# Seven products for the gates and the next values of an mLSTM layer

## Chip, cores and metric

The kernel runs on one core of a Trainium2 chip. The metric is device time in microseconds (us). The kernel before takes 2154.1 us, the median of three runs (2154.06 to 2154.34).

## What is computed

Two layers of an encoder, for 256 positions of width 2048, in float32. Layer 0 mixes by pooling and attention, layer 1 by an mLSTM with 8 heads of 256, and each is followed by a gated MLP with a convolution over positions. The change is in the mixer of layer 1. Cut to what matters, and with both directions in one formula, it is:

```
xn = rms_norm(x, g)                                  # 256 x 2048
q, k, v, o, gates = split(xn @ w_in)                 # 4 x 2048 columns, and 32 for the gates' pre-activations
for each head h (256 columns):
    A = sum over directions of  (q_h k_h^T * decay) / max(|row sum|, bound)      # 256 x 256
    y_h = rms_norm(A @ v_h) * sigmoid(o_h)
x = x + concat(y_h) @ w_out
```

`v` and `o` (the output gates) are thus two products of the same `xn` with two sets of weight columns.

## The kernel before, in words

**Products.** Every large product is made of tiles of 128 rows (K tiles, 16 for a width of 2048) by 512 columns. Both factors are split in a high and a low part that TensorE multiplies at its fp32r rate, and a product takes three matmuls: high by high, high by low, low by high. A group `mv` (values of two heads, 512 columns, 256 positions in two halves t) or `mo` (their gates) takes 16 K tiles x 2 halves x 3 = 96 matmuls into one PSUM tile of the pool `mm`. `mq` and `mk` (queries and keys of one head, L374) have the weights as the stationary side and work likewise.

**Weights.** All weights stream through one list of chunks of 128 x 1024 (512 KB, two K tiles of 512 columns), class Stream. SP loads a chunk into one of 7 buffers `w`, ahead of its use; ACT casts it to the high part (L134) and DVE subtracts that for the low part (L135), into one of 4 buffers `hl`. A chunk of `mo` or `mv` is used by 12 matmuls. The cast of a chunk can start once the last matmul of the chunk four places ahead of it, which used the same buffer, is done.

**Seven products before the change.** The down products of both MLPs (tile `pp`) already go in seven products of half-sized blocks rather than eight, as Strassen's rule does. Their sums of weights are made by DMA in DRAM, by `premix` (L475, tile `m`): per mix two copies are issued by ACT and three accumulating transfers by POOL, each in two halves, paced by the latest matmul. `Made` chunks of the stream are loaded from these sums.

**The mLSTM layer** (from L766). For each pair of heads hp: the values `mv`; for each of its two heads `mq` and `mk`, and a task `head`; then the gates `mo`, and a task `gated`. The order on PE is that of the code. Tasks are Python generators that the class Weave (L161) runs between the matmuls once a given amount of matmul time has gone by, so that small work of one head stands between the large matmuls of what follows. ACT and DVE take their instructions in an order that a scheduler sets when the program is built.

The task `head` issues 12 matmuls `qk`; on DVE four multiplications by the decay, which also sum rows (L882), three small ones for the reciprocal of the bound (L885 to L887) and four that build the matrix `A` (L889 to L892); then four transposes of `A` on PE (`atr`, L898), their split (`at`, L900 and L901), and 12 matmuls `av`. The task `gated` makes the sigmoid of the gates in the tile `og` (ACT exponential L923, DVE addition L927 and reciprocals L929), multiplies the head's normed result by it (L933) and transposes that (`htr`, L938). Both heads' `head` tasks and the `gated` task of a pair run beside the following large groups: the second head's beside `mo` and the next pair's `mv`.

Of the kernel before, what the change touches and what calls it, by code (L numbers as in the profile page):

```python
# [9 lines left out]
F32 = mybir.dt.float32  # L10
F32R = mybir.dt.float32r
AF = mybir.ActivationFunctionType
# [4 lines left out]
P = 128  # L17
D = 2048
# [198 lines left out]
def trunk(ctx: ExitStack, tc: tile.TileContext, gx, xT, xn, call, catt, cml, weights, mixes, out):  # L217
# [555 lines left out]
    def mlstm_layer(norm, nxt):  # L773
        with ExitStack() as es:
# [145 lines left out]
            def gated(ps, heads):  # L920
                og = t1p.tile([P, 2, len(heads) * MD], F32, tag="og", name=f"og{heads[0]}")
                for t in range(2):
                    a.activation(og[:, t, :], ps[:, t, :], AF.Exp, scale=nrcol[:, t : t + 1])  # L923
                yield 1.2
                for i, h in enumerate(heads):
                    o = og[:, :, i * MD : i * MD + MD]
                    v.tensor_scalar_add(o, o, 1.0)  # L927
                    for t in range(2):
                        tc.keep_in_program_order(v.reciprocal(o[:, t], o[:, t]))  # L929
# [3 lines left out]
                    tc.keep_in_program_order(v.tensor_mul(hn, hn, o))  # L933
# [11 lines left out]
                    done.add(h)  # L945

            hns, done = {}, set()
            wv.add(norm.finish(), 6.0)
            for hp in range(MH // 2):
                vf = t1p.tile([P, 2, 512], F32, tag="vf", name=f"mvf{hp}")  # L950
                for c, n in ((0, MD + 32), (MD, MD)) if hp == 0 else ((0, 512),):
                    ps = mov_group(xx, f"mv{hp}_{c}", n)
                    if hp + c == 0:
                        wv.until(lambda: norm.rcol is not None)
                        wv.add(gates(ps))
                    n = min(n, 512 if hp else MD)
                    for t in range(2):
                        a.activation(vf[:, t, c : c + n], ps[:, t, :n], AF.Copy, scale=norm.rcol[:, t : t + 1])
# [12 lines left out]

            def ready(i):
                wv.until(lambda: set(range(6 + 2 * i)) <= done)
# [4 lines left out]
    def ffn_layer(layer, norm, nxt):  # L978
        with ExitStack() as es:
# [229 lines left out]
def _mov(w):  # L1209

    return w.reshape(-1, 2, P, 512).transpose(0, 2, 1, 3).reshape(-1, P, CH * P)
# [18 lines left out]


def _ml_chunks(w_in, w_out):
    a = []
    for hp in range(MH // 2):
        c = 2 * D + hp * 512
        a.append(_mov(w_in[:, c : c + 512]) if hp else _stat(w_in[:, c + MD : c + 512], range(KT)))
# [5 lines left out]
        a.append(_mov(wo))  # L1242
    return np.concatenate(a), _out_chunks(w_out, ML_PARTS)


def _up_chunks(w):
# [56 lines left out]
    return seq + [("down", c, b) for b in range(2, NB)]  # L1303


def _down_chunks(layer, w):
# [12 lines left out]
    res = [np.concatenate(out)]  # L1319

    def two(a, b):
        return np.concatenate([a, b], axis=2)

    for h in range(2):
        b = w[: 2 * n * P, 1024 * h : 1024 * h + 1024].reshape(n, 2, P, 2, 512)
        b11, b12, b21, b22 = (b[:, k, :, c] for k in range(2) for c in range(2))
        res += [two(b12, b12), two(b11, b22), two(b22, b21), two(b11, b21), two(b22[::2], b22[1::2])]
    return res


# [130 lines left out]
```

## Time and profile before

| | |
|---|---|
| median of 3 runs | 2154.1 us |
| profiled execution, its time | 2154.6 us |
| profiled execution, its span | 2152.7 us |
| PE busy | 2147.7 us, 11400 matmuls |
| DVE, ACT, POOL busy | 1760.0, 1420.2, 250.2 us |
| DMA | 578.31 MB, mean 269 GB/s |

The span is the time from the first to the last instruction of the profiled execution; 1.9 us of its time lie outside. "Busy" counts the time in which an engine executes; PE's matmuls overlap, so that the distance from one to the next is shorter than a matmul's own duration. In an answer of the profile, `out<-in` names the tiles that an instruction writes and reads, and xN counts them. L272 is the one line that issues all large matmuls, so groups are told apart by tile. The chain of waits follows the work that ended last back through whatever released it.

### The profile page before, as it was taken

The page shows a single profiled execution, that of the slowest core. Times are in us where ns is not written, and L with a number is a line of the kernel's source. Part 1 is how long each engine was busy: PE and PEld are TensorE (multiplying, and loading weights), DVE is VectorE, ACT ScalarE, POOL GpSimd, SP SyncE. Part 2 cuts the span into 40 slices and gives each one's busy share as a digit, 9 for nine tenths or more (in the row PEclk, how much of TensorE's full clock was granted, in tenths as well). Part 3 has the DMA queues.
Part 4 walks back from the last instruction along what each step waited for, and adds up shares of the span by engine and source line. Part 5 has one row for each costly group of instructions (what it writes and reads, how often), then busy time and mean ns, then how long its engine had stood idle before and what let it go on. Part 6 is the DMA issues. An engine that isn't in the chain of part 4 may idle for free.

```text
span 2152.7 us, 32117 instructions
## 1 busy us (share of the span) xinstructions
PE 2147.7 (100%) x11400; PEld 1842.3 (86%) x11400; DVE 1760.0 (82%) x2468; ACT 1420.2 (66%) x2171; POOL 250.2 (12%) x318
## 2 busy tenths in 40 slices
PE   9999999999999999999999999999999999999999
PEld 8888888888888888889888888888888888888887
DVE  7786678889988999897777677667888998889988
ACT  6665577777777777666554544457777777777774
POOL 0022112111111110001111111111111000000000
PEclk9999999999999999999999999999999999999999
DMA  9678889899999997778788888988989888778775
GB/s 332 209 213 255 261 250 323 269 328 331 317 330 328 315 287 257 264 259 250 227 252 247 244 247 229 286 240 253 298 280 285 281 266 255 268 254 269 253 250 186
DMA packets 172226, 578.31 MB, mean 269 GB/s; under 512 B 22074, under 2 KB 24930, under 8 KB 172066
## 3 DMA queue, kind: packets, MB, share of 16 engines
q1 hardware_dynamic: 131360, 469.16, 61.3%
q0 software_dynamic: 24544, 61.10, 17.0%
q10 hardware_dynamic: 16162, 46.01, 6.6%
q8 instruction: 89, 1.46, 0.3%
q14 instruction: 71, 0.58, 0.1%
HBM read 574.04 MB, written 86.03 MB: 307 GB/s over the span
## 4 chain that ended last, share of the span: by engine, by line
PE 98%; DVE 1%; issue 0%; ACT 0%; ACTq 0%; DVEq 0%
PE up L272 45%; PE pp L272 16%; PE op L272 8%; PE mv L272 4%; PE mq L272 4%; PE mk L272 4%; PE mo L272 4%; PE qproj L272 3%; PE dn L272 3%; PE kproj L272 1%; PE vproj L272 1%; PE pool L272 1%; PE av L272 1%; PE qk L272 1%; PE xt L323 0%; DVE hl L135 0%
## 5 line engine op out<-in xcount | busy, mean ns | idle before, releaser
L135 DVE TENSOR_TENSOR hl<-w,hl 128x1024 fp32r<-128x1024 f32 (+1 forms) x851 | 1024.0, 1215 | 196.0 <-ACT hl L134 186.1
L134 ACT CAST hl<-w 128x1024 fp32r<-128x1024 f32 (+1 forms) x850 | 872.4, 1046 | 420.6 <-PE up L272 121.5
L272 PE MATMUL up<-xx,hl 128*128 128x512 f32 (+1 forms) x5632 | 993.6, 337 | 0.0
L272 PEld LDWEIGHTS up<-xx,hl 128*128 128x128 f32 x5632 | 867.2, 188 | 129.8
L272 PE MATMUL pp<-hl,s 128*128 128x512 f32 x912 | 226.5, 390 | 0.2
L484 POOL DMA_DIRECT2D m<-m x160 | 128.3, 820 | 798.2 <-PE up L272 304.0
L272 PEld LDWEIGHTS pp<-hl,s 128*128 128x128 f32 x912 | 168.1, 188 | 34.2 <-DVE hl L135 1.4
L272 PE MATMUL pp<-hl,g 128*128 128x512 f32 x684 | 173.9, 390 | 0.0
L272 PEld LDWEIGHTS pp<-hl,g 128*128 128x128 f32 x684 | 125.9, 188 | 24.3
L438 ACT COPY tb_up<-up 128x512 f32<-128x512 f32 x88 | 51.7, 587 | 123.0 <-PE up L272 123.0
L484 POOL DMA_DIRECT2D m<-in_dn x80 | 71.0, 888 | 357.1 <-PE dn L272 121.2
L1010 DVE TENSOR_TENSOR y<-y,z 128x510 f32<-128x510 f32 x88 | 60.7, 689 | 60.2 <-ACT y L1009 60.1
L1009 ACT ACTIVATE y<-tb_up,conv 128x256 f32<-128x256 f32 x176 | 103.7, 589 | 0.0
L439 DVE TENSOR_TENSOR tb_up<-up,tb_up 128x512 f32<-128x512 f32 x88 | 60.8, 691 | 40.6 <-ACT tb_up L438 40.2
L272 PE MATMUL mk<-xx,hl 128*128 128x512 f32 (+1 forms) x512 | 92.2, 337 | 0.0
L272 PE MATMUL mq<-xx,hl 128*128 128x512 f32 (+1 forms) x512 | 92.2, 337 | 0.0
L272 PE MATMUL mv<-hl,xx 128*128 128x512 f32 (+2 forms) x480 | 91.8, 351 | 0.0
L272 PE MATMUL op<-hl,cat 128*128 128x512 f32 x384 | 91.5, 393 | 0.0
L272 PE MATMUL mo<-hl,xx 128*128 128x512 f32 x384 | 90.5, 391 | 0.0
L1007 ACT ACTIVATE z<-tb_up,conv 128x256 f32<-128x256 f32 x176 | 88.3, 502 | 3.2 <-DVE tb_up L1002 2.3
L272 PE MATMUL op<-hl,mcat 128*128 128x512 f32 x384 | 89.5, 392 | 0.0
L272 PEld LDWEIGHTS mq<-xx,hl 128*128 128x128 f32 x512 | 79.2, 188 | 11.6
(233 smaller groups left out, 2135.8 us busy)
## 6 DMA issues: line engine op xcount, KB each, us to landing
w<-in_up SPq DMA_DIRECT2D x352, 512.0 KB, 5.8
w<-in_dn SPq DMA_DIRECT2D x174, 512.0 KB, 5.1
w<-in_m_in SPq DMA_DIRECT2D x124, 512.0 KB, 5.2
m<-in_dn ACTq DMA_DIRECT2D x160, 256.0 KB, 5.9
w<-m SPq DMA_DIRECT2D x80, 512.0 KB, 4.8
w<-in_a_in SPq DMA_DIRECT2D x45, 512.0 KB, 5.6
m<-in_dn POOLq DMA_DIRECT2D x80, 256.0 KB, 7.0
m<-m POOLq DMA_DIRECT2D x160, 128.0 KB, 5.8
```

The costliest lines, as they stand in the source:

```text
L134: (self.nc.vector.tensor_copy if i + c == 0 else self.nc.scalar.copy)(hl[:, 0, c : c + n], w[:, c : c + n])
L135: low = self.nc.vector.tensor_sub(hl[:, 1, c : c + n], w[:, c : c + n], hl[:, 0, c : c + n].bitcast(F32))
L272: last_mm[0] = pe.matmul(out_, lhsT, rhs, start=start, stop=stop, skip_group_check=True)
L438: a.copy(tb, ps[:, :, 1, :])
L439: v.tensor_add(tb, ps[:, :, 0, :], tb)
L484: paced(eng.dma_start(to[p : p + P // 2], src[p : p + P // 2], **kw))
L1007: a.activation(z[:, 0, j, :], u[:, j, :], AF.Copy, scale=cw(tl, 0))
L1009: a.activation(y[:, j, :], u[:, j, :], AF.Identity, scale=cw(tl, 1), bias=cw(tl, 3))
L1010: v.tensor_add(y[:, :, 1:S], y[:, :, 1:S], z[:, 0, :, 0 : S - 1])
```

## The change

For the pairs hp = 0, 1 and 2 a new function `gates_values(hp)` makes the gates of pair hp and the values of pair hp + 1 together, as one product with 1024 columns, in the place where `mo` and the next `mv` stood. The first pair's values and the last pair's gates are made as before.

K tiles 0 to 7 go in four pairs. In each pair the two halves of the positions, the two K tiles and the two sets of 512 columns form a 2 x 2 by 2 x 2 product, which takes seven products (21 matmuls) rather than eight (24). Four of the seven have a sum of blocks of `xn` as stationary factor, and one of the others is added directly into `mo`. K tiles 8 to 15 go directly, two parts of `mo` (ML_DIRECT) and the end of `mv`. A pair of heads thus takes 180 large matmuls rather than 192.

What is new beside these matmuls:

- the tile `mcomb` with the sums of blocks of `xn`, high and low part, made once by a task `combos`, five DVE instructions and one ACT cast for each of four pairs of K tiles;
- the PSUM tiles `mp46`, `mp5` and `mp0`, and the tasks `first` and `second`, which add them up in the SBUF tiles `og` and `vf`: two ACT copies, eight DVE instructions of 512 columns, and two more that add `mv` to `vf`. The task `gated` starts behind `second` and reads `og`;
- 22 chunks of weights rather than 16 for each of the three pairs. 14 of them are used by 6 matmuls each and 8 by 12;
- 12 mixes of a third list, `premix(2)`, for the sums of weights of these chunks. They start in the first MLP, where c = 3 and i = 6. The 20 mixes of the second MLP, `premix(1)`, no longer start at c = 5 and i = 4 of the first MLP, but behind the first pair in the mLSTM layer.

Line numbers shift by 2 or 3: the matmuls stand in L274, the cast in L136, the low part in L137, the task `head`'s lines in 885 to 904.

The diff, without the functions that cut and list the weights on the host:

```
+ML_PAIRS = 4
+ML_DIRECT = (list(range(2 * ML_PAIRS, 12)), list(range(12, KT)))
...
+            comb = actp.tile([P, ML_PAIRS, 2, 4, P], F32R, tag="B1", name="mcomb")
...
+            def combine(j):
+                f = tp.tile([P, 2, S], F32, tag="hn", name=f"mf{j}")
+                pair = norm.xx[:, 2 * j : 2 * j + 2]
+                v.tensor_add(f, pair[:, :, 0].bitcast(F32), pair[:, :, 1].bitcast(F32))
...
+                v.tensor_sub(sf[:, 0:2], g4[:, 0::3], g4[:, 1:2].to_broadcast([P, 2, P]))
+                v.tensor_add(sf[:, 2], sf[:, 1], g4[:, 0])
+                v.tensor_sub(sf[:, 3], g4[:, 2], sf[:, 2])
+                a.copy(comb[:, j, 0], sf)
+                v.tensor_sub(comb[:, j, 1], sf, comb[:, j, 0].bitcast(F32))
...
+            def gates_values(hp):
+                og = t1p.tile([P, 2, 512], F32, tag="og", name=f"og{2 * hp}")
+                vf = t1p.tile([P, 2, 512], F32, tag="vf", name=f"mvf{hp + 1}")
+                x00, x10, x01, x11 = og[:, 0], og[:, 1], vf[:, 0], vf[:, 1]
+                wv.until(lambda: "combos" in done)
...
+                direct(mo, ML_DIRECT[0], (True, True), (False, False))
...
+                for j in js:
+                    xs = [[comb[:, j, i, m] for i in range(2)] for m in (1, 0, 2)] + [x_part(2 * j + 1, 1)]
+                    for n, (ps, x_) in enumerate(zip((p46[:, 0], p46[:, 1], p5, mo[:, 1]), xs)):
+                        if n % 2 == 0:
+                            hl = st.next()
+                        wh, wl = (hl[:, i, n % 2 * 512 : n % 2 * 512 + 512] for i in range(2))
+                        product(ps, x_, wh, wl, n < 3 and j == 0, n < 3 and j == js[-1])
...
+                wv.add(first(), 0.3)
+                direct(mo, ML_DIRECT[1], (False, False), (False, True))
+                p0 = psp.tile([P, 512], F32, tag="ps", name=f"mp0{hp}")
+                for j in js:
+                    hl = st.next()
+                    for n, ps in enumerate((p0, mo[:, 0])):
+                        wh, wl = (hl[:, i, n * 512 : n * 512 + 512] for i in range(2))
+                        product(ps, x_part(2 * j + n, 0), wh, wl, n == 0 and j == 0, j == js[-1])
...
+                wv.add(second(), 0.3)
+                mv = mmp.tile([P, 2, 512], F32, tag="mm", name=f"mv{hp + 1}")
+                for j in js:
+                    if j % 2 == 0:
+                        hl = st.next()
+                    wh, wl = (hl[:, i, j % 2 * 512 : j % 2 * 512 + 512] for i in range(2))
+                    product(mv[:, 0], [comb[:, j, i, 3] for i in range(2)], wh, wl, j == 0, False)
+                for n, kts in enumerate(ML_DIRECT):
+                    direct(mv, kts, (False, n == 0), (n == 1, n == 1))
+                wv.until(lambda: f"g{hp}" in done)
+                for t in range(2):
+                    v.tensor_add(vf[:, t], vf[:, t], mv[:, t])
+                    a.activation(vf[:, t], vf[:, t], AF.Copy, scale=norm.rcol[:, t : t + 1])
+                return vf
...
-                wv.add(gated(mov_group(xx, f"mo{hp}"), [2 * hp, 2 * hp + 1]))
+                if hp < MH // 2 - 1:
+                    vf = gates_values(hp)
+                else:
+                    wv.add(gated(mov_group(xx, f"mo{hp}"), [2 * hp, 2 * hp + 1]))
+                hp == 0 and premix(1, 30.0, 30.0, 0)
...
-                    if layer == 0 and c == len(FCH) - 1 and i == 4:
-                        premix(1, 30.0, 30.0, 0)
+                    if layer == 0 and (c, i) == (len(FCH) - 3, 6):
+                        premix(2, 30.0, 30.0, 0)
```

**Place 1, PE, from the start of the gates of pair 0.** Before, `mo` is the gates, and qk and atr belong to the second head of the pair; the number behind `hl` is the chunk.

```order
L272 MATMUL mo_10207<-hl_10157,xx_2446 128x512 x12
L272 MATMUL mo_10207<-hl_10178,xx_2446 128x512 x12
L272 MATMUL mo_10207<-hl_10210,xx_2446 128x512 x12
L272 MATMUL qk_10271<-hl_k_10204,hl_q_10071 128x256 x12
L272 MATMUL mo_10207<-hl_10237,xx_2446 128x512 x12
L272 MATMUL mo_10207<-hl_10256,xx_2446 128x512 x12
L898 MATMUL atr_10334<-cst,A_10293 128x128 x4
```

The same place on PE now; mp is one of the new PSUM tiles mp46 and mp5.

```order
L274 MATMUL mo_10320<-hl_10267,xx_2446 128x512 x12
L274 MATMUL mo_10320<-hl_10291,xx_2446 128x512 x12
L274 MATMUL mp_10366<-hl_10323,mcomb 128x512 x6
L274 MATMUL qk_10379<-hl_k_10315,hl_q_10181 128x256 x12
L274 MATMUL mp_10367<-hl_10351,mcomb 128x512 x3
L274 MATMUL mo_10320<-hl_10351,xx_2446 128x512 x3
L274 MATMUL mp_10366<-hl_10370,mcomb 128x512 x6
L274 MATMUL mp_10367<-hl_10408,mcomb 128x512 x3
L274 MATMUL mo_10320<-hl_10408,xx_2446 128x512 x3
L274 MATMUL mp_10366<-hl_10419,mcomb 128x512 x6
L901 MATMUL atr_10452<-cst,A_10401 128x128 x4
```

Between qk and atr stood 24 matmuls of two chunks; now 24 matmuls of four chunks stand there, the last of them chunk hl_10419.

**Place 1, DVE, the same head's work between qk and atr.** Before (arg is the decay, den and denr the bounds):

```order
L135 TENSOR_TENSOR hl_10318<-w_10208,hl_10318 128x1024
L882 SCALAR_TENSOR_TENSOR arg_10223,den_10284<-qk_10271,arg_10223 128x128
L882 SCALAR_TENSOR_TENSOR arg_10223,den_10284<-qk_10271,arg_10223 128x256 x2
L882 SCALAR_TENSOR_TENSOR arg_10223,den_10284<-qk_10271,arg_10223 128x128
L885 SCALAR_TENSOR_TENSOR denr_10289<-den_10284 128x4
L886 TENSOR_TENSOR denr_10289<-denr_10289,mc 128x4
L887 RECIPROCAL denr_10289<-denr_10289 128x4
L889 TENSOR_SCALAR A_10293<-arg_10223,denr_10289 128x256
L891 TENSOR_SCALAR A_10293<-arg_10223,denr_10289 128x256
L890 SCALAR_TENSOR_TENSOR A_10293<-arg_10223,denr_10289,A_10293 128x128
L892 SCALAR_TENSOR_TENSOR A_10293<-arg_10223,denr_10289,A_10293 128x128
L135 TENSOR_TENSOR hl_10344<-w_10235,hl_10344 128x1024
```

Now, from the end of the multiplications on:

```order
L888 SCALAR_TENSOR_TENSOR denr_10397<-den_10392 128x4
L137 TENSOR_TENSOR hl_10432<-w_10349,hl_10432 128x1024
L889 TENSOR_TENSOR denr_10397<-denr_10397,mc 128x4
L137 TENSOR_TENSOR hl_10443<-w_10368,hl_10443 128x1024
L890 RECIPROCAL denr_10397<-denr_10397 128x4
L137 TENSOR_TENSOR hl_10462<-w_10406,hl_10462 128x1024
L892 TENSOR_SCALAR A_10401<-arg_10332,denr_10397 128x256
L894 TENSOR_SCALAR A_10401<-arg_10332,denr_10397 128x256
L137 TENSOR_TENSOR hl_10473<-w_10417,hl_10473 128x1024
L893 SCALAR_TENSOR_TENSOR A_10401<-arg_10332,denr_10397,A_10401 128x128
L895 SCALAR_TENSOR_TENSOR A_10401<-arg_10332,denr_10397,A_10401 128x128
```

The eleven instructions of the head stood together; now four low parts of chunks stand among them, the last (hl_10473) ahead of the two that finish `A`. Chunk hl_10473 is the fourth behind hl_10419 (hl_10432, hl_10443 and hl_10462 lie between). Pairs 1 and 2 have the same order.

**Place 2, DVE, the sigmoid of the gates.** Before, behind the end of `mo`:

```order
L927 TENSOR_SCALAR og_10435<-og_10435 128x2x256 x2
L929 RECIPROCAL og_10435<-og_10435 128x256 x2
L135 TENSOR_TENSOR hl_10450<-w_10342,hl_10450 128x1024
L929 RECIPROCAL og_10435<-og_10435 128x256
L135 TENSOR_TENSOR hl_10468<-w_10359,hl_10468 128x1024
L135 TENSOR_TENSOR hl_10489<-w_10405,hl_10489 128x1024
L933 TENSOR_TENSOR hn_10137<-hn_10137,og_10435 128x512
```

Now, from the sums of the task `second` on; hl_10656 is the last chunk of `mv`, and from hl_10677 on the chunks are of the next pair's `mq`:

```order
L1033 TENSOR_TENSOR mvf_10319<-mvf_10319,mp_10563 128x512
L137 TENSOR_TENSOR hl_10656<-w_10597,hl_10656 128x1024
L1033 TENSOR_TENSOR mvf_10319<-mvf_10319,mp_10563 128x512
L137 TENSOR_TENSOR hl_10677<-w_10610,hl_10677 128x1024
L930 TENSOR_SCALAR og_10318<-og_10318 128x2x256 x2
L137 TENSOR_TENSOR hl_10696<-w_10623,hl_10696 128x1024
L932 RECIPROCAL og_10318<-og_10318 128x256 x3
L137 TENSOR_TENSOR hl_10724<-w_10635,hl_10724 128x1024
L1049 TENSOR_TENSOR mvf_10319<-mvf_10319,mv_10609 128x512 x2
L936 TENSOR_TENSOR hn_10247<-hn_10247,og_10318 128x512
```

The reciprocals stood among the low parts of `mv`; now they stand behind the sums, among those of the next `mq`.

More of the change, by code (lines that the diff above doesn't have):

```diff
@@ new lines, in combos, with product, x_part @@
+            def combos():
+                for j in range(ML_PAIRS):
+                    yield from wv.wait(lambda: norm.blocks > j // 2)
+                    combine(j)
+                    yield 8.0
+                done.add("combos")
+            def product(ps, xs, wh, wl, first, last):
+                xh, xl = xs
+                mm(ps, xh, wh, first, False)
+                mm(ps, xh, wl, False, False)
+                mm(ps, xl, wh, False, last)
+                wv.tick(0.68)
+            def x_part(k, t):
+                return [norm.xx[:, k, i, t * P : t * P + P] for i in range(2)]
@@ L1232, in _ml_chunks @@
 def _ml_chunks(w_in, w_out):
-    a = []
+    c = 2 * D
+    a, made = [_stat(w_in[:, c + MD : c + 512], range(KT))], [[], [], []]
+    k0, k1 = 2 * ML_PAIRS * P, ML_DIRECT[1][0] * P
     for hp in range(MH // 2):
-        c = 2 * D + hp * 512
-        a.append(_mov(w_in[:, c : c + 512]) if hp else _stat(w_in[:, c + MD : c + 512], range(KT)))
         for h in (2 * hp, 2 * hp + 1):
@@ L1241, in _ml_chunks, with _ml_weights, some @@
         wo = w_in[:, 3 * D + hp * 512 : 3 * D + hp * 512 + 512]
-        a.append(_mov(wo))
-    return np.concatenate(a), _out_chunks(w_out, ML_PARTS)
+        if hp == MH // 2 - 1:
+            a.append(_mov(wo))
+            continue
+        wv = w_in[:, 2 * D + hp * 512 + 512 : 2 * D + hp * 512 + 1024]
+        s0, s1, r, ba, bb = _seven(np.concatenate([wo[:k0], wv[:k0]], axis=1))
+        for to, e in zip(made, (s0, s1, r)):
+            to.append(e)
+        a += [_mov(wo[k0:k1]), _mov(wo[k1:]), ba, bb, _mov(wv[k0:])]
+    return np.concatenate(a), _out_chunks(w_out, ML_PARTS), [np.concatenate(e) for e in made]
+def _ml_weights(chunks, parts):
+    chunks, mixes = iter(chunks), []
+    def some(n):
+        return [next(chunks) for _ in range(n)]
+    out = some(KT // 4)
+    for hp in range(MH // 2):
+        out += some(KT)
+        if hp == MH // 2 - 1:
+            out += some(KT // 2)
+            continue
+        out += some(len(ML_DIRECT[0]) // 2)
+        for j in range(ML_PAIRS):
+            made = [Made(), Made()]
+            mixes.append([p[hp * ML_PAIRS + j] for p in parts] + [made])
+            out += made
+        out += some(len(ML_DIRECT[1]) // 2 + ML_PAIRS + ML_PAIRS // 2 + (KT - 2 * ML_PAIRS) // 2)
+    return out, mixes
 def _up_chunks(w):
@@ L1303, in _ffn_plan, with _seven, two @@
     return seq + [("down", c, b) for b in range(2, NB)]
+def _seven(w):
+    def two(a, b):
+        return np.concatenate([a, b], axis=2)
+    b = w.reshape(-1, 2, P, 2, 512)
+    b11, b12, b21, b22 = (b[:, k, :, c] for k in range(2) for c in range(2))
+    return [two(b12, b12), two(b11, b22), two(b22, b21), two(b11, b21), two(b22[::2], b22[1::2])]
 def _down_chunks(layer, w):
@@ L1319, in _down_chunks @@
     res = [np.concatenate(out)]
[L1321 to L1322 removed]
     for h in range(2):
[L1325 to L1327 removed]
+        res += _seven(w[: 2 * n * P, 1024 * h : 1024 * h + 1024])
     return res
@@ L1433 @@
     }
+    arrays.update({f"m_s{j}": part for j, part in enumerate(m_made)})
     for l in range(2):
@@ L1454 @@
     vg = [t["m_g"][:, c : min(c + n, m_g.shape[1])] for c in range(0, m_g.shape[1], n)]
-    weights = chunks("a_in") + chunks("a_out") + ffn(0) + vg + chunks("m_in") + chunks("m_out") + ffn(1)
+    m_weights, m_mixes = _ml_weights(chunks("m_in"), [chunks(f"m_s{j}") for j in range(3)])
+    weights = chunks("a_in") + chunks("a_out") + ffn(0) + vg + m_weights + chunks("m_out") + ffn(1)
+    mixes.append(m_mixes)
     with tile.TileContext(nc, schedule_with_timeline_sim=True) as tc:
```

55 lines of the change are left out of this document (43 added, 12 removed).

## The prediction

> **What bounds the kernel now.** I read the page first, then the chain of waits, then the busy time by windows over the three stretches that the change touches, and in them the groups and the timeline.
>
> ```profile
> PE 2147.7 (100%) x11400; PEld 1842.3 (86%) x11400; DVE 1760.0 (82%) x2468; ACT 1420.2 (66%) x2171; POOL 250.2 (12%) x318
> PE   9999999999999999999999999999999999999999
> POOL 0022112111111110001111111111111000000000
> PEclk9999999999999999999999999999999999999999
> PE 98%; DVE 1%; issue 0%; ACT 0%; ACTq 0%; DVEq 0%
> ```
>
> PE is busy in 2147.7 of 2152.7 us, in every slice, at full granted clock, and 98% of the chain is PE. Time is lost or won only by matmuls that go or by stalls of PE. PE is as full in the slices in which POOL makes sums of weights (1 or 2) as in those without (0).
>
> One large matmul's price is read from the chain, where a piece is time from start to start, not from its own duration, which overlaps with the next:
>
> ```profile
> 1065.01 13.60 PE mv L272 x60
> 1160.81 13.60 PE mv L272 x60
> 1256.61 13.60 PE mv L272 x60
> ```
>
> 13.60 / 60 = 0.2267 us for each of 512 columns. A chunk used by 12 matmuls thus lasts 2.72 us on PE, one used by 6 only 1.36.
>
> The three stretches of `mo` and the next `mv`, and the one behind the first of them, by windows (columns: PE, PEld, DVE, ACT and POOL busy, granted clock, DMA share, GB/s):
>
> ```profile
> 1039.60:1087.10 47.50, 47.50 (x226) 39.76 (x226) 35.52 (x54) 22.63 (x30) 7.03 (x9) 1.00 0.83 245
> 1135.40:1182.90 47.50, 47.50 (x226) 39.76 (x226) 35.60 (x54) 22.51 (x30) 7.05 (x9) 1.00 0.82 238
> 1231.00:1278.70 47.70, 47.70 (x227) 39.93 (x226) 35.09 (x55) 22.62 (x30) 7.24 (x9) 1.00 0.80 238
> 1087.00:1111.00 24.00, 24.00 (x141) 20.95 (x140) 13.88 (x15) 13.31 (x17) 3.92 (x5) 1.00 0.85 246
> ```
>
> PE has no gap in them; DVE has 12 us to spare in each.
>
> **The matmuls that go.** Three pairs of heads times 192 - 180 = 12 matmuls, 36 in all: 36 x 0.2267 = 8.16 us. This is all that the change takes from PE.
>
> **The work that DVE and ACT get.** From the groups of the first stretch, and from the additions of the down products, whose form (512 columns, one operand in PSUM) is that of the new ones:
>
> ```profile
> L135 DVE TENSOR_TENSOR hl<-w,hl 128x1024 fp32r<-128x1024 f32 x16 | 19.2, 1211 | 6.4 <-ACT hl L134 6.3
> L134 ACT CAST hl<-w 128x1024 fp32r<-128x1024 f32 x16 | 16.8, 1053 | 19.5 <-PE mo L272 9.1 <-PE mv L272 6.7 <-DVE hn L933 2.4
> L929 DVE RECIPROCAL og<-og 128x256 f32<-128x256 f32 x4 | 6.8, 1733 | 0.0
> ```
>
> ```profile
> L1087 DVE TENSOR_TENSOR acc<-acc,pp x64: 676/680/685, 447.7 to 2125.5; 128x512 f32<-128x512 f32 x64
> L1085 ACT COPY acc<-pp x16: 566/582/588, 330.8 to 1563.0; 128x512 f32<-128x512 f32 x16
> its engine sat idle before it (us, times) until:
>   DVE hl L135: 1.4, 3
> ```
>
> A stretch gets six more chunks and ten more additions. DVE: 35.5 + 6 x 1.21 + 10 x 0.68 = 49.6 us of work for 47.5 - 12 x 0.2267 = 44.8 us of PE. ACT: 22.6 + 6 x 1.05 + 2 x 0.58 = 30.1 us, which fits. DVE's 4.8 us too many can go only into what follows, and the window from 1087 has 24.00 - 13.88 = 10.1 us free. Place 2 of the order shows that this is where the reciprocals (6.8 us) now stand. I count the overflow at nothing; without that cover it is the second rival.
>
> **The wait that the order makes.** At place 1, PE reaches the transposes `atr` of a pair's second head right after chunk hl_10419. The first needs L893, which DVE has behind the low part of hl_10473. The cast of hl_10473 needs the buffer of hl_10419, so it cannot start until PE has finished the very matmuls before `atr`. In before nothing of the kind stood there:
>
> ```profile
> L898 PE MATMUL atr<-cst,A x32: 270/272/273, 1028.0 to 1342.5; 128*128 128x128 f32 x32
> ```
>
> ```profile
> 1049.26 5.64 PE L272 MATMUL mo<-hl,xx 128*128 128x512 f32 x24
> 1052.14 0.35 DVE L889 TENSOR_SCALAR A<-arg,denr 128x256 f32<-128x256 f32 x1
> 1052.21 1.05 ACT L134 CAST hl<-w 128x1024 fp32r<-128x1024 f32 x1 [3.08 <-PE mo L272]
> 1052.41 0.35 DVE L891 TENSOR_SCALAR A<-arg,denr 128x256 f32<-128x256 f32 x1
> 1052.67 0.35 DVE L890 SCALAR_TENSOR_TENSOR A<-arg,denr,A 128x128 f32<-128x128 f32 x1
> 1052.94 0.34 DVE L892 SCALAR_TENSOR_TENSOR A<-arg,denr,A 128x128 f32<-128x128 f32 x1
> 1053.30 1.23 DVE L135 TENSOR_TENSOR hl<-w,hl 128x1024 fp32r<-128x1024 f32 x1
> 1054.44 1.40 DVE L869 SCALAR_TENSOR_TENSOR arg<-G,mc,kml 128x128 f32<-128x128 f32 x4
> 1054.51 0.58 PEld L898 LDWEIGHTS atr<-cst,A 128*128 128x128 f32 x4
> 1054.74 0.60 PE L898 MATMUL atr<-cst,A 128*128 128x128 f32 x4
> ```
>
> `A` was complete at 1053.28 and `atr` came at 1054.74: 1.5 us in hand. From these rows the new wait is worked out, counted from the end of hl_10419's last matmul. The 24 matmuls from 1049.26 are two chunks; the first ends at 1049.26 + 2.72 = 1051.98, and the cast that waits for it starts at 1052.21: 0.23 us. The cast takes 1.05, so it ends at 1.28. DVE comes from the cast of the chunk before (hl_10462), released 1.36 us earlier: its low part starts at about -0.08, the next instruction 1.14 us later (1053.30 to 1054.44), and two halves of `A` take 0.27 each (1052.14 to 1052.67 for two), so DVE is free at 1.60. Then the low part, 1.14, and L893, 0.35: 3.1 us. The weights of a transpose are loaded 0.23 us ahead of it (1054.51 to 1054.74): 3.3 us. The last of the four needs L895, which is done at 3.4, and stands 0.45 us behind the first: no more. I take **3.3 us, three times, 9.9 us**. Ends: 2.8 if DVE is free when the cast ends and nothing is paid for loading weights, 4.0 if DVE is another half low part behind. Queued behind `atr` on PE is everything; the splits of the next four chunks are done meanwhile, so none is late after it.
>
> ACT and DVE take their instructions strictly in order, says the Trainium skill ("TensorE: Matmul & The Clock Gate", "Architectural detail"), and PE may pull only loads of weights ahead. By that rule the stall stands; if the two halves of `A` could pass hl_10473 it would vanish, and the sum would be 2146. In the rows above every instruction of DVE starts behind the one before.
>
> **Edits that I cost at nothing or little.**
>
> `combos`: four times five DVE instructions, two of 512 columns (0.68 each, as L1087), one of 256 (0.35, as L891) and two of 128 (at most that), some 2.4 us each time, at the layer's start. In the row below DVE has 4.8 of 13 us free, before that none (6.00 of 6.00), so a step of the start can be late.
>
> ```profile
> 966.00:972.00 6.00, 6.00 (x49) 6.00 (x48) 6.00 (x15) 4.41 (x11) 0.78 (x1) 1.00 0.74 221
> 972.00:985.00 13.00, 13.00 (x106) 13.00 (x105) 8.17 (x15) 7.44 (x12) 1.51 (x2) 1.00 0.91 179
> ```
>
> I take 0.5 us for that and for the transposes `htr`, which come behind the moved reciprocals; ends 0 and 2.4, one set of `combos` in full.
>
> Loads: six more of 512 KB for each pair, which raises the stretch from 245 to about (245 x 47.5 + 6 x 524) / 44.8 = 330 GB/s.
>
> ```profile
> w<-in_m_in SPq DMA_DIRECT2D x124, 512.0 KB, 5.2
> w<-m SPq DMA_DIRECT2D x80, 512.0 KB, 4.8
> GB/s 332 209 213 255 261 250 323 269 328 331 317 330 328 315 287 257 264 259 250 227 252 247 244 247 229 286 240 253 298 280 285 281 266 255 268 254 269 253 250 186
> ```
>
> Slices of the first MLP run at 330 with PE full, so this fits. Loads land in 5.2 us, and six chunks ahead are 8.2 us even where each lasts 1.36: hidden, at nothing. Were it gone, one load would be late by up to 5.2 us.
>
> Short chunks as such: `pp` lives on chunks of 6 matmuls too and waited for low parts three times, 1.4 us in all. But there they alternate with long ones, and here eight come in a row. At 1.36 us each they leave the cast (1.05) and the low part (1.14) just room; that is why anything put between them, as at place 1, is paid.
>
> The mixes: 12 more, in the first MLP (four copies on ACT's queue and six accumulating transfers on POOL's for each). The 20 of the second MLP start behind the first pair, about 1087, where before the first seven copies were issued from 860 to 960, so 130 to 230 us later. The rows of DMA issues in the windows 860 to 960, 1600 to 1700 and 1950 to 2100:
>
> ```profile
> m<-in_dn ACTq DMA_DIRECT2D x7, 256.0 KB, 5.0
> ```
>
> ```profile
> m<-m POOLq DMA_DIRECT2D x10, 128.0 KB, 5.8
> ```
>
> ```profile
> w<-m SPq DMA_DIRECT2D x12, 512.0 KB, 4.7
> ```
>
> The last sums were made before 1700 and would be by 1930, and the chunks of the last six mixes are loaded from 1950 on: in time. By the page's slices PE doesn't feel such transfers: nothing. If a load did have to wait for its sum, the wait would show whole.
>
> **The sum**, against the profiled execution's 2154.6: - 8.16 + 9.9 + 0.5 = 2156.8. That execution lies 0.5 above the median, so the forecast is **2156.3 us**. Of the ends: - 8.2 + 8.4 + 0 gives 2154.3, - 8.2 + 12.0 + 2.4 gives 2160.3.
>
> **Rivals.**
>
> 1. *No stall: the change does its sum.* Then 2154.1 - 8.2 = 2146, up to 2148 with the small terms. It needs `A` done ahead of `atr`, as in before, where 1.5 us were in hand. Against it: the chain above has no link that depends on a duration being long; even its shortest form is 2.8 us.
>
> 2. *DVE's overflow reaches PE (slower).* The place is the end of the stretch, where reciprocals and sums stand among low parts. If the low parts are already late there, PE waits for each, and the 49.6 - 44.8 = 4.8 us are paid for each pair in place of 3.3 or with part of it: 3 x 4.8 = 14.4, 2154.1 - 8.2 + 14.4 = 2160.3. It decides once the low part of the last `mv` chunk or of the first `mq` chunk ends behind PE's need of it. For it: DVE is short by more than the stall gives back. Against it: `mv` ends with four long chunks (10.9 us of PE for 4.6 us of low parts), and the stall itself lets DVE catch up by 3.3 us.
>
> 3. *The clock falls at the stalls.* Before shows no pause of PE in which this could be seen, only PEclk at 9 throughout. If the clock were halved after each stall for as long as the stall, it would cost 3 x 3.3 / 2 = 5.0 us more: 2161.3. The Trainium skill ("TensorE: Matmul & The Clock Gate", "HAM oscillation") says that gaps of PE over about 3.4 us halve the clock, and that the window runs freely; by its "What's actually happening" the whole window must be idle, which a pause of 3.3 us doesn't fill, and by that the sum stays.
>
> **How the numbers follow.** My forecast has 0.62, rival 1 has 0.08, rival 2 0.22, rival 3 0.03, and 0.05 is for a late load or sum of weights, or more. About 0.2% (4.3 us) is what a measurement of this kernel can tell from no change: faster is below 2149.8, slower above 2158.4. Rival 1 is faster, 0.08. Of the forecast's range 2154.3 to 2160.3 the larger part lies below 2158.4: 0.52 of 0.62, and with it a part of rival 2 where only some of the overflow is paid, 0.04: same 0.56. The rest is slower: 0.36. The range leaves out rival 1 and the worst: 2152.5 to 2162.
>
> **What would show it.** In the profile after: `atr` in pairs 0 to 2 with PE idle about 3.3 us before it, released by DVE's L893 or L895, and a gap of that length between mp46's matmuls and `atr`; 36 fewer matmuls; DVE over 95% busy in the stretch, and the same PE period elsewhere. If PE instead waits before `mv` or `mq` matmuls for `hl` L137, rival 2 holds. PEclk below 9 in these slices would show rival 3. The forecast is wrong at its root if `atr` shows no idle time; that DVE's order or the four buffers were read wrongly would be the reason.

## The result, and the profile after

The changed kernel takes 2161.76 us (median of 6 runs, 2160.82 to 2163.09) against 2154.16 before: the ratio is 1.0035, 95% interval 1.0022 to 1.0048. It is slower, by 7.6 us, where I forecast 2.2 more and called it no change; the time lies just within the range.

The page of the profile after, whose own time is 2162.26 us:

```profile
span 2160.5 us, 32447 instructions
PE 2144.7 (99%) x11364; PEld 1837.2 (85%) x11364; DVE 1804.7 (84%) x2536; ACT 1445.4 (67%) x2199; POOL 305.4 (14%) x390
PEclk9999999999999999999999999999999999999999
PE 92%; DVE 3%; DMA 2%; issue 1%; ACT 1%; ACTq 0%; DVEq 0%; SPq 0%
```

11400 - 11364 = 36 matmuls are gone, as the change says. PE is now idle for 15.8 us, and the chain is no longer PE alone: 3% is DVE and 2% DMA. The clock's digits show nothing: 3.4 us at half clock leave the mean of a slice of 54 us at 0.97. What PE waited for:

```profile
PE atr L901 <- DVE A L893: 8.9, 3, 3.0
PE wps L298 <- DVE pad L702: 1.2, 1, 1.2
PE pp L274 <- DVE hl L137: 1.0, 1, 1.0
PE mk L274 <- DVE hl L137: 0.6, 1, 0.6
PE htr L941 <- DVE hn L936: 0.2, 1, 0.2
```

Only `wps` stood there before:

```profile
PE wps L296 <- DVE pad L700: 1.2, 1, 1.2
```

To see where the time comes from I compare the first starts of the same tiles (the answer per tile has min/median/max of the duration, then first and last start), before and then after:

```profile
L272 PE MATMUL up<-xx,hl x5632: 273/336/580, 256.4 to 2103.5; 128*128 128x512 f32 x98, 128*128 128x256 f32 x97
L272 PE MATMUL mv<-hl,xx x480: 278/389/486, 965.1 to 1278.5; 128*128 128x512 f32 x96, 128*128 128x288 f32 x32, 128*128 128x256 f32 x32
L272 PE MATMUL mo<-hl,xx x384: 387/389/476, 1039.7 to 1352.0; 128*128 128x512 f32 x192
L272 PE MATMUL op<-hl,mcat x384: 387/389/486, 1352.2 to 1442.9; 128*128 128x512 f32 x192
```

```profile
L274 PE MATMUL up<-xx,hl x5632: 273/387/580, 256.2 to 2111.3; 128*128 128x512 f32 x98, 128*128 128x256 f32 x97
L274 PE MATMUL mv<-hl,xx x336: 279/297/390, 967.1 to 1285.5; 128*128 128x512 f32 x72, 128*128 128x288 f32 x48, 128*128 128x256 f32 x48
L274 PE MATMUL mo<-hl,xx x312: 387/390/629, 1042.5 to 1359.9; 128*128 128x512 f32 x156
L274 PE MATMUL op<-hl,mcat x384: 387/390/486, 1360.1 to 1450.8; 128*128 128x512 f32 x192
```

So the first MLP (up to mv) went from 708.7 to 710.9, the start of the mLSTM layer (mv to mo) from 74.6 to 75.4, and the rest of that layer with its three changed stretches (mo to op) from 312.5 to 317.6: + 2.2, + 0.8 and + 5.1, with - 0.3 elsewhere the 7.8 us by which the span grew. The first was at nothing in my sum, the second stood there with 0.5, and of the third my sum had 9.9 - 8.2 = 1.7.

The stall that was. The timeline of the first stretch:

```profile
1054.84 1.52 PE L274 MATMUL mp<-hl,mcomb 128*128 128x512 f32 x6
1056.40 1.04 ACT L136 CAST hl<-w 128x1024 fp32r<-128x1024 f32 x1 [0.30 <-PE mp L274]
1057.27 0.35 DVE L892 TENSOR_SCALAR A<-arg,denr 128x256 f32<-128x256 f32 x1
1057.53 0.35 DVE L894 TENSOR_SCALAR A<-arg,denr 128x256 f32<-128x256 f32 x1
1057.80 1.22 DVE L137 TENSOR_TENSOR hl<-w,hl 128x1024 fp32r<-128x1024 f32 x1
1058.93 0.34 DVE L893 SCALAR_TENSOR_TENSOR A<-arg,denr,A 128x128 f32<-128x128 f32 x1
1059.33 0.95 PE L901 MATMUL atr<-cst,A 128*128 128x128 f32 x4 [2.97 <-DVE A L893]
1059.94 1.63 PE L274 MATMUL mp<-hl,mcomb 128*128 128x512 f32 x3
1061.36 1.48 PE L274 MATMUL mo<-hl,xx 128*128 128x512 f32 x3
```

Chunk's end, cast, the rest of A's first halves, low part, L893, `atr`: the chain of the prediction, 2.97 us long. The last two rows show something else: three matmuls take 1.63 and 1.48 us, and the next piece starts 1.42 us after the first; three take 0.68 elsewhere. The windows (busy time of PE, of PEld, which is PE's loading of weights, of DVE, ACT and POOL; then granted clock, DMA share, GB/s) say why:

```profile
1055.00:1059.30 4.30, 1.36 (x7) 0.78 (x5) 4.25 (x8) 2.10 (x2) 0.00 (x0) 1.00 0.98 202
1059.30:1061.00 1.70, 1.67 (x7) 1.48 (x8) 1.67 (x6) 0.59 (x1) 0.00 (x0) 0.57 1.03 414
1061.00:1063.00 2.00, 2.00 (x6) 1.59 (x5) 0.63 (x1) 0.91 (x2) 0.00 (x0) 0.51 1.02 410
1063.00:1066.00 3.00, 3.00 (x19) 2.64 (x18) 1.72 (x2) 2.52 (x3) 0.77 (x1) 1.00 0.53 180
```

```profile
1251.00:1255.10 4.10, 1.22 (x6) 0.68 (x4) 4.05 (x8) 2.00 (x2) 0.25 (x1) 1.00 0.90 227
1255.20:1257.20 2.00, 2.00 (x11) 1.74 (x12) 1.97 (x6) 0.91 (x2) 0.00 (x0) 1.00 0.87 338
1257.20:1259.20 2.00, 2.00 (x11) 1.63 (x10) 0.57 (x2) 1.93 (x3) 0.00 (x0) 1.00 1.02 416
```

Behind the stall of pair 0 the granted clock is half, for some 3.4 us, and then full again; behind that of pair 2, as long, it stays full. Pair 1 is like pair 0: half from 1158.5 to 1161.9. Two halvings cost 2 x 3.4 / 2 = 3.4 us. The three stretches then add up: - 8.2 + 8.9 + 0.2 + 3.4 = + 4.3 of the 5.1; 0.8 us stay spread over small pieces.

**Theory**: the order at `atr` makes the stall, the stall halves the clock, and the mixes in the first MLP delay its loads. **Rival**: DVE is simply short in the stretches, so that a wait which is taken away comes back.

### The profile page after: what moved, and what is told of

Read it like the earlier page. It is cut to its first block, busy times and chain, and to the rows that moved or that the text cites. A ratio compares the mean times of both kernels' runs of the same rounds, so it can differ in the third digit from the quotient of the medians.

```text
span 2160.5 us, 32447 instructions
## 1 busy us (share of the span) xinstructions
PE 2144.7 (99%) x11364; PEld 1837.2 (85%) x11364; DVE 1804.7 (84%) x2536; ACT 1445.4 (67%) x2199; POOL 305.4 (14%) x390
## 4 chain that ended last, share of the span: by engine, by line
PE 92%; DVE 3%; DMA 2%; issue 1%; ACT 1%; ACTq 0%; DVEq 0%; SPq 0%
PE up L274 43%; PE pp L274 15%; PE op L274 8%; PE mk L274 4%; PE mq L274 3%; PE mo L274 3%; PE qproj L274 3%; PE dn L274 3%; PE mv L274 2%; DVE hl L137 2%; PE mp L274 1%; PE kproj L274 1%; PE vproj L274 1%; DMA w<-in_dn 1%; PE pool L274 1%
## 5 line engine op out<-in xcount | busy, mean ns | idle before, releaser
L137 DVE TENSOR_TENSOR hl<-w,hl 128x1024 fp32r<-128x1024 f32 (+1 forms) x869 | 1047.3, 1217 | 173.3 <-ACT hl L136 161.2
L136 ACT CAST hl<-w 128x1024 fp32r<-128x1024 f32 (+1 forms) x868 | 890.8, 1045 | 398.4 <-PE up L274 110.8
L274 PE MATMUL up<-xx,hl 128*128 128x512 f32 (+1 forms) x5632 | 994.1, 337 | 0.1
L274 PEld LDWEIGHTS up<-xx,hl 128*128 128x128 f32 x5632 | 867.6, 188 | 130.1 <-DVE hl L137 0.9
L486 POOL DMA_DIRECT2D m<-m x208 | 166.4, 817 | 943.0 <-PE up L274 428.5
L274 PE MATMUL pp<-hl,s 128*128 128x512 f32 x912 | 227.0, 391 | 1.3 <-DVE hl L137 1.0
L274 PEld LDWEIGHTS pp<-hl,s 128*128 128x128 f32 x912 | 168.0, 188 | 35.9 <-DVE hl L137 3.3
L274 PE MATMUL pp<-hl,g 128*128 128x512 f32 x684 | 174.0, 390 | 0.0
L274 PEld LDWEIGHTS pp<-hl,g 128*128 128x128 f32 x684 | 125.9, 188 | 24.4
L274 PE MATMUL mk<-xx,hl 128*128 128x512 f32 (+1 forms) x512 | 93.2, 338 | 0.6 <-DVE hl L137 0.6
L274 PE MATMUL mq<-xx,hl 128*128 128x512 f32 (+1 forms) x512 | 92.2, 338 | 0.0
L274 PE MATMUL op<-hl,cat 128*128 128x512 f32 x384 | 91.6, 393 | 0.0
L1118 ACT ACTIVATE z<-tb_up,conv 128x256 f32<-128x256 f32 x176 | 88.2, 501 | 3.9 <-DVE tb_up L1113 2.0
L274 PEld LDWEIGHTS mk<-xx,hl 128*128 128x128 f32 x512 | 79.2, 189 | 12.3 <-DVE hl L137 1.0
L274 PE MATMUL op<-hl,mcat 128*128 128x512 f32 x384 | 89.5, 392 | 0.0
L274 PEld LDWEIGHTS mq<-xx,hl 128*128 128x128 f32 x512 | 79.3, 188 | 11.6
L1119 ACT ACTIVATE z<-tb_up,conv 128x256 f32<-128x256 f32 x176 | 87.3, 496 | 0.0
```

Of the source, the lines that this page charges most:

```text
L136: (self.nc.vector.tensor_copy if i + c == 0 else self.nc.scalar.copy)(hl[:, 0, c : c + n], w[:, c : c + n])
L137: low = self.nc.vector.tensor_sub(hl[:, 1, c : c + n], w[:, c : c + n], hl[:, 0, c : c + n].bitcast(F32))
L274: last_mm[0] = pe.matmul(out_, lhsT, rhs, start=start, stop=stop, skip_group_check=True)
L486: paced(eng.dma_start(to[p : p + P // 2], src[p : p + P // 2], **kw))
L1118: a.activation(z[:, 0, j, :], u[:, j, :], AF.Copy, scale=cw(tl, 0))
L1119: a.activation(z[:, 1, j, :], u[:, j, :], AF.Copy, scale=cw(tl, 2))
```

## The experiments

Each time is beside runs of the kernel before on the same chip (2154.0 to 2154.3). The runs of one kernel spread over 2 to 8 us, those of before over 0.3 to 3, so medians tell 1 to 2 us apart at best; finer readings are of one profile each, by the three spans from start to start.

| kernel | median us | ratio, interval | up to mv | mv to mo | mo to op |
|---|---|---|---|---|---|
| before | 2154.2 | | 708.7 | 74.6 | 312.5 |
| changed | 2161.8 | 1.0022 to 1.0048 | 710.9 | 75.4 | 317.6 |
| a_first | 2154.7 | 0.9992 to 1.0011 | 712.7 | 76.4 | 307.9 |
| fill | 2160.3 | 1.0019 to 1.0038 | 710.2 | 76.0 | 314.5 |
| mix_only | 2157.1 | 1.0005 to 1.0024 | 711.9 | 74.5 | 312.6 |
| mix_mid | 2159.2 | 1.0014 to 1.0033 | 709.1 | 76.0 | 313.9 |
| pin_av | 2150.2 | 0.9971 to 0.9990 | 710.7 | 76.0 | 305.0 |
| combos_late | 2161.9 | 1.0023 to 1.0051 | 713.6 | 75.9 | 316.2 |
| best_mid | 2151.9 | 0.9980 to 0.9998 | 709.1 | 76.4 | 308.4 |
| best2 | 2150.7 | 0.9977 to 0.9995 | 709.1 | 76.8 | 307.0 |
| best3 | 2155.2 | 0.9998 to 1.0016 | 709.1 | 83.5 | 306.5 |
| fill4 | one run, 2162.8 | | 712.9 | 75.8 | 316.0 |
| best4 | 2153.7 | 0.9990 to 1.0008 | 709.1 | 79.8 | 306.5 |
| combos_only | 2154.4 | 0.9995 to 1.0013 | 708.6 | 74.6 | 312.5 |

**a_first.** The low part of the third chunk to be split after A's instructions is issued is tied behind them:

```
+                last = v.scalar_tensor_tensor(A[:, 1, P:S], ...)
+                if hh == 1 and h < 6:
+                    st.pin = st.n_split + 2, last
...
+            if self.pin and i >= self.pin[0]:
+                self.behind(low, self.pin[1])
+                self.pin = None
```

> The changed kernel with one order on DVE pinned: at the second head of pairs 0 to 2 the four instructions that build A stand together ahead of the low part of hl_10432 (and its like), as they did before the change; nothing else is touched. Theory (the atr wait is made by the order, and it drags the clock down): PE no longer waits at atr (8.9 us gone) and the granted clock stays 1.00 (3.4 us gone), 2161.8 - 12.3 = about 2149.5. Rival (DVE is 4.8 us short in each stretch, and atr is only where that shows first): waits for hl come back in the same stretch, 3 us or so for each pair, and the time stays at 2158 to 2162.

Measured 2154.7. PE's waits in its three stretches:

```profile
PE av L278 <- DVE at L910: 2.3, 3, 0.8
```

`atr` no longer waits, the clock is full everywhere in this profile, and the three stretches lose 9.7 us. That is less than the 12.3 expected, because `av` now comes 0.8 us too early three times. The total is 5 us above the expectation: besides the 2.3 us, in this profile the first MLP lost 4.0 rather than 2.2, and the layer's start 1.8 rather than 0.8.

**pin_av.** As a_first, and `av` comes later (`yield 4.6` for `yield 3.2` ahead of it in these heads).

> The changed kernel with A's instructions kept together on DVE (as in a_first) and the 12 matmuls av of the same heads issued 1.4 us of matmul time later. Theory (in a_first the remaining 2.3 us, three waits of 0.8 us of av for the split of at, are only av's place): no wait in the three stretches, mo of pair 0 to the output product in about 312.5 - 8.2 + 1 = 305 us, and the total 2154.7 - 2.3 = 2152.4, if the first MLP loses as much as in a_first. Rival (DVE is short, and each wait that goes comes back further on): a wait for hl or at of 0.5 to 1 us in each stretch again, at another place, and the total stays at 2154.7.

Measured 2150.2: faster than before. All of PE's waits:

```profile
PE mk L278 <- DVE hl L138: 1.3, 1, 1.3
PE wps L302 <- DVE pad L706: 1.2, 1, 1.2
PE pp L278 <- DVE hl L138: 0.7, 3, 0.3
```

None is in the stretches, though DVE's work there is the same. They take 7.5 us less than before, of the 8.16 that the matmuls are worth. Where DVE's surplus went, by windows of its first stretch and of the one behind it:

```profile
1042.80:1087.40 44.60, 44.60 (x212) 37.28 (x211) 40.56 (x61) 28.85 (x37) 6.89 (x10) 1.00 0.98 315
1087.40:1111.00 23.60, 23.60 (x141) 20.72 (x140) 20.63 (x24) 13.48 (x19) 3.21 (x5) 1.00 0.80 224
```

40.56 us in the stretch and 20.63 behind it, where it was 13.88: about 7 us have moved there, and PE has no gap in either. In this kernel the rival falls.

**fill and fill4.** Ten, or four, matmuls ahead of the late `atr`, their results not used:

```
                 tr = psp.tile([P, 2, S], F32, tag="ps", name=f"atr{h}")
+                if hh == 1 and h < 6:
+                    for _ in range(10):
+                        mm(tr.rearrange("p a b -> p (a b)"), x_part(0, 0)[0], ..., True, True)
```

> The changed kernel with ten matmuls of 512 columns more ahead of the three late atr, into the PSUM tile that atr then overwrites; their results are not used. They take 2.3 of the 3.0 us in which PE stood idle. Theory (the clock falls because PE stands idle for 3.0 us): the time until atr is the same, the granted clock stays 1.00 behind it, 2161.8 - 3.4 = about 2158.4. Rival (the clock falls for another reason, such as what follows the wait): 2161.8 or a little more, with the clock at 0.5 in the 3 us behind atr in some of the three places.

```profile
PE atr L904 <- DVE A L893: 2.1, 3, 0.7
```

PE reaches `atr` no earlier, yet the stretches are 3.1 us shorter than in the changed kernel, and the clock is full behind all three. So it is the pause that halves the clock. The median, 2160.3, is 1.5 below the changed kernel's rather than 3.4; its runs spread from 2158.3 to 2164.2.

> As fill, with four matmuls of 512 columns in place of ten: they fill the first 0.9 us of the 3.0, so that PE then stands idle for 2.1 us. It tells how long a pause the clock takes. Theory (a pause near the length of the low-clock stretch, 3.4 us, is needed): granted clock 1.00 behind all three, 3 us less than the changed kernel in the three stretches. Rival (about 2 us are enough): a stretch of 3.4 us at 0.50 behind one or more of the three.

Here PE stands idle for 2.1 us at each of the three. Behind the third:

```profile
1255.00:1258.00 3.00, 3.00 (x9) 2.32 (x8) 1.31 (x4) 2.23 (x3) 0.00 (x0) 0.52 1.00 406
```

One of three pauses of 2.1 us is enough, so the theory's "near 3.4 us" is wrong.

**mix_only.** The kernel before, with only the mixes of the change added and moved; the 12 sums are not used.

```
+                hp == 0 and premix(1, 30.0, 30.0, 0)
...
-                    if layer == 0 and c == len(FCH) - 1 and i == 4:
-                        premix(1, 30.0, 30.0, 0)
+                    if layer == 0 and (c, i) == (len(FCH) - 3, 6):
+                        premix(2, 30.0, 30.0, 0)
...
```

> The kernel before, with the 12 mixes for the mLSTM weights made in DRAM where the changed kernel makes them, and the 20 of the second MLP started where it starts them; the 12 sums are not used, all products are those of before. Theory (the first MLP loses 2.2 us because the new transfers delay loads there): 2154.2 + 2.2 = 2156.4, lost between 680 and 760 us. Rival (the loss in the first MLP is not from the mixes): 2154.2.

Measured 2157.1, and the span up to mv is 3.2 us longer, the rest unchanged. The mixes do cost. Of the DMA issues from 690 to 760 us, first before, then after the change:

```profile
w<-in_up SPq DMA_DIRECT2D x16, 512.0 KB, 6.6
w<-in_dn SPq DMA_DIRECT2D x10, 512.0 KB, 8.2
```

```profile
w<-in_up SPq DMA_DIRECT2D x16, 512.0 KB, 8.7
w<-in_dn SPq DMA_DIRECT2D x9, 512.0 KB, 10.0
m<-in_m_s ACTq DMA_DIRECT2D x8, 256.0 KB, 6.8
```

The loads land 2 us later, while the mixes of both sets run. Six chunks of 1.36 us ahead would cover 8.2 us; here chunks of `up` (64 matmuls in 11.1 us from four of them) stand between those of `pp`, so the cover is longer than that. But single loads are later than the medians: the chain of waits after, which before was PE alone at this place, goes back to one of 14.93 us and one of 10.62:

```profile
708.23 14.93 DMA w<-in_dn
...
723.23 10.62 DMA w<-in_up
...
746.19 1.45 PE pp L274 x5
```

**mix_mid.** The changed kernel with its 12 mixes later: `(c, i) == (len(FCH) - 2, 4)` and `premix(2, 24.0, 24.0, 0)`.

> The changed kernel, with the 12 mixes started later in the first MLP (c = 4, i = 4, where the mixes of its own down products are nearly done), one every 24 us of matmul time rather than 30. Theory (two sets of mixes at a time are too much for the loads): the loss in the first MLP goes, 2161.8 - 2.0 = 2159.8. Rival (12 mixes cost that wherever they run beside an MLP): the same 2161.8, with the wait moved behind 800 us.

Measured 2159.2; its profile is of its fastest run, 2157.0. It has 709.1 up to mv: 0.4 us lost rather than 2.2, with no wait in the first MLP, as in the four later kernels with the same late mixes (best2, best3, best4 and best_mid, 709.1 each). It is two sets of mixes at a time that are too much. Its three stretches are 3.7 us shorter than the changed kernel's as well: a different order on ACT and DVE left one pair without the stall at `atr`, and one halving in place of two.

**combos_late, combos_only, best3 and best4** were to find the 0.8 us of the layer's start. The first starts `combos` at 34.0 in place of 16.0.

> The changed kernel with the task combos started 34 rather than 16 us after the start of the mLSTM layer, so that its DVE work stands beside the queries and keys of pair 0 rather than beside the gates' rows. Theory (combos delay the gates' rows and with them the loads of G, behind which DVE's low parts stand): mk's wait of 0.6 us goes, and from the first mv to the first mo 74.6 us as before the change, not 75.4; total 2161.0. Rival (mk's wait is from the slower DMA of gd and G, not from combos): 75.4 stays, total 2161.8.

75.9 us from mv to mo, 2161.9 in all: nothing gained, and `qk` now waits twice for `hl_k`, 0.7 us each.

> As best2, and the task combos starts 34 us after the layer's start with its first addition pinned behind what DVE was given before, so that it really stands behind the gates' rows on DVE. Theory (combos among the gates' rows delay G, and mk then waits for low parts that stand behind G's readers): mk's wait of 0.6 to 1.3 us goes, 2147.6. Rival (the work is only moved, in front of head 0's hl_k or A): as much waiting at qk or atr of head 0, 2148.4 or more.

It pins the first addition (`tc.keep_in_program_order(v.tensor_add(f, ...))`). 83.5 us: the work stands in front of head 0's `A`, and `atr` waits 3.8 us with the clock at half behind it. The rival here, and worse.

> As best2, with the five additions of each of the four combos on POOL in place of DVE, behind what POOL was given before them. Theory (it is DVE's work for combos that makes the start of the mLSTM layer late, 2 us from the first mv to the first mo in best2): this time falls from 76.8 to about 75 us, total 2149. Rival (the start is late for something else, such as the cast of combos on ACT or slower transfers of the gates' rows): 76.8 stays, total 2150.7 or more.

The additions go to POOL (`g.tensor_sub` for `v.tensor_sub`, and so on). 79.8 us: worse, for a reason of its own (last section).

> The kernel before with the task combos of the changed kernel added at the start of the mLSTM layer; its result is not used. Theory (combos alone make the start late): from the first mv to the first mo 75.4 to 76.8 us in place of 74.6, total 2155.0 to 2156.4, with PE waiting at mk or gtr. Rival (the start is late for something else, such as the mixes beside it or the further loads ahead): 74.6, total 2154.2.

The kernel before with `combos` alone: 74.6 us, 2154.4. So neither `combos` alone nor the mixes alone make the start late; with both, and the rest of the change, it is later by 0.8 to 2.2 us in each kernel whose `combos` stay on DVE unpinned. How they do it together is open. What the traces show is that the reader of `G` (L869, now L872), behind which DVE's low parts queue, starts later: 39.7 us behind the first mv before, and 43.0 after.

**best_mid and best2** put repairs together: pin_av and mix_mid, and in best_mid combos_late too.

> All four repairs: A together on DVE, av later, the 12 mixes later in the first MLP with one every 24 us, combos later. Theory (the sum of the parts): 2154.2 - 8.2 (matmuls) + 1 (small pieces in the stretches) + 0.4 (what the mixes still cost) = about 2147.4, faster than both kernels, with no wait of PE over 0.5 us. Rival (DVE short by 4.8 us in each stretch, or the mixes cost 2 us wherever they run): 2149.5 to 2155, with the waits in the trace.

> Three repairs: A together on DVE, av later, the 12 mixes later in the first MLP; combos as in the changed kernel. Theory (the parts add): pin_av's 2150.2 less the 1.5 to 2 us that its first MLP lost, about 2148.4, faster than the kernel before by 0.2 to 0.3%; waits of PE only at the start of the mLSTM layer, 1 to 1.5 us. Rival (the mixes cost the same wherever they run, only at another place): 2150.

2151.9 and 2150.7: both beat both kernels, but not by the sum. The 2 us of the first MLP are won in both (709.1). In best2 1.4 of them go again to one wait of `htr` for `hn` that pin_av doesn't have, and 0.8 at the start; in best_mid two waits of `qk`, 0.7 each, and others of 0.3 to 0.6. pin_av at 2150.2 and best2 at 2150.7 can't be told apart; they are 0.20% and 0.14% faster than before.

## Why the prediction was right, and where it was wrong

- *The matmuls, - 8.16 us*: right. 36 fewer, and pin_av, with no wait left there, takes 7.5 us less in the three stretches. 0.7 us of small pieces remain unexplained.
- *The wait at atr, 9.9 us*: right in place, cause and number; 8.9 us, 3.0 each rather than 3.3. I had charged 0.23 us for loading weights, of which the wait shows nothing. a_first shows that the order alone made it, so that it was no price of seven products.
- *DVE's overflow at nothing*: right. pin_av shows the 7 us in the stretch behind. The sign that I named for it failed: DVE is not over 95% busy in the first stretch but 83% (40.67 of 49.1 us), and 91% in pin_av. Rival 2 had 0.22 and shows neither in the changed kernel nor in pin_av; best_mid, best3 and best4 have waits of `mv` for a low part, of 0.3 us or less.
- *The mixes at nothing*: the step that failed. I read "PE doesn't feel such transfers" from slices in which one set of mixes ran, and checked that the sums would be ready in time; that they would run beside another set, at a place where loads took 6.6 to 8.2 us already and single ones then took 10.6 and 14.9, I didn't weigh. It cost 2.2 us in the profile after and 3.2 in mix_only. The bound that I named for a late load, 5.2 us, would have covered it.
- *Rival 3, the clock*: named with its price per stall (1.7 us) but given 0.03. By the Trainium skill ("TensorE: Matmul & The Clock Gate", "What's actually happening") the clock falls after a whole idle window, which a pause of 3.3 us doesn't fill; that rule came between me and the answer. The clock fell behind two of three stalls, 3.4 us. My sign for it, PEclk below 9 in the page's slices, could not have shown it: a slice is too long.
- *The start, 0.5 us*: 0.8 with `htr`'s 0.2 beside it; the mechanism I named (DVE has no room for `combos`) isn't what combos_only shows.

So the likeliest case came with its own terms nearly right (- 8.2 + 8.9 + 1.0), and two mechanisms that I had priced at nothing or nearly so (+ 2.2 and + 3.4) made "no change" into "slower". That the time still lies in the range, by 0.2 us, is luck: it is beyond 2160.3, the end of my own sum, and the two mechanisms that carried it there stood in the sum at nothing.

## What to carry to other kernels

Where a change halves the time that a chunk lasts, look through the order of every engine for a short chain that now stands behind a buffer's release: here one tie of order and one later slot turned + 7.6 us into - 4. A stall of PE should be priced with the half-clock stretch that can follow it. And work that is moved to a quiet engine still takes DMA: compare the loads' landing time with what the buffers cover, at the tightest place that it runs beside.

## What the runs showed of the hardware

**Pauses and the clock.** Over all profiles, in the mLSTM layer, the granted clock fell to 0.50 at 5 of 7 pauses of 3.0 us, 1 of 3 of 2.1 us, one of 3.8 us (best3) and one of 1.8 us that came soon after one of 1.0 (best4), and at none of the single ones of 0.7 to 1.6 us. A pause of 2 to 3 us thus costs 1.7 us more or it doesn't. This can part two runs of one kernel, but it isn't all of their spread: a_first's runs of 2151.4 and 2157.8 both have a mean clock of 1.00. The fall came between 0.3 us before PE went on and 1.4 us after it, and lasted about 3.4 us. In best3 it came within the pause (from 1030.96 to 1034.76) and lasted 6.8 us:

```profile
1033.00:1037.00 4.00, 2.24 (x9) 2.05 (x10) 4.00 (x11) 1.75 (x4) 0.00 (x0) 0.50 0.96 306
1037.00:1040.00 3.00, 3.00 (x11) 2.57 (x11) 1.53 (x3) 1.86 (x2) 0.00 (x0) 0.53 0.30 94
```

The Trainium skill ("TensorE: Matmul & The Clock Gate", "HAM oscillation") puts the limit at pauses of about 3.4 us; its length of a window agrees with the low stretches, its limit doesn't: 2.1 us were enough once.

Which pause is followed by a fall can be worked out from the same traces, though no run tested it. The two falls of the changed kernel (1059.55 and 1158.53) lie 98.98 us apart and those of combos_late (1157.52 and 1256.51) 98.99, which is 29 times 3.413, as if the clock were set anew only every 3.41 us. Counted back and forth from a fall in steps of that length, PE was idle for 1.84 to 2.97 us in the step just before each of the eight falls, and for at most 1.89 us in any other step from 250 us on in those six profiles. So the second pause of the changed kernel, which lay with 0.96 us in one step and 2.01 in the next, was followed by a fall, and the third, with 1.89 and 1.08, was not. The limit, by this estimate, is some 1.9 us of idle time within one step, and the same pause costs more or nothing by where it happens to lie.

**POOL beside DVE.** In best4, while POOL made its additions, two scans of DVE that took 0.68 us each before were slower:

```profile
995.56 2.26 DVE L829 TENSOR_TENSOR_SCAN rows_b<-rows_b 8x256 f32<-8x256 f32 x1
995.75 1.52 POOL L960 TENSOR_TENSOR mf<-xx 128x512 f32<-128x512 f32 x1
997.84 1.07 DVE L830 TENSOR_TENSOR_SCAN rows_b<-rows_b 8x256 f32<-8x256 f32 x1
```

2.26 and 1.07 us: work given to POOL was paid by DVE. The low part that began at 1014.62, with POOL busy for 3.42 of the 3.50 us from there, took 3.45 us rather than 1.22; `mq` waited 1.84 us for it, and the clock fell behind that pause. The two waits of `mq`, 2.8 us in all, and the 1.7 us of the fall, less 1.4 us of waits that best2 has there, give 3.1 us; best4's start is 3.0 later than best2's. The slower DVE instructions agree with the Trainium skill ("GPSIMD Engine Reference", "1. Specifications"), by which POOL shares its interfaces to SBUF with DVE and the two contend where a DVE instruction has two inputs there.
